# One layer of a hybrid encoder on one core: the order of the mix's plain halves, the slots of the late embeddings, and the steps at which finished quarters are passed on

## The chip, the core and the metric

The kernel runs on one core of a Trainium2 chip. The metric is the device time of one execution in microseconds (us); lower is better. The times of the runs of the kernel before are given as their median, and one more execution was taken with the hardware profiler: all rows shown below come from it. Engine names: PE is TensorE (matmuls and transposes), DVE is VectorE, ACT is ScalarE, POOL is GpSimd, SP is SyncE, whose queue issues most of the loads.

## What is computed

All in float32, for 512 tokens of width 2048, one layer:

```
qA|kA|vA|qB|kB|vB = x @ w_in
A = windowed attention, 8 heads, with sinks        B = dilated attention, 8 heads, three patterns
mix = concat(rms_norm(A), rms_norm(B)) @ w_o
h   = layer_norm(alpha * x + mix, ln1)
ff  = square(relu(h @ w1)) @ w2                    # 2048 -> 8192 -> 2048
ple = (p @ w_ple) * sigmoid(h @ w_ple_gate)
out = layer_norm(alpha * h + ff + ple, ln2)
```

## The kernel before

**Tiles.** Each float32 product is made of three matmuls: both operands are split into a high and a low part (wh, wl of the weights, s1h, s1l and so on of the features), ACT making the high part by a rounding copy and DVE the low part by a subtraction (lines 87 and 88 for weights, 433 and 434, put, for features). One matmul takes 128 x 128 features and 128 x 512 weights into a PSUM bank.

**Stages.** Attention and projections go first; the heads' results are scaled by a spread norm factor (line 327, after PE's line 307) and stored in DRAM as y_d (line 329). Then the embeddings of the first two column groups (embed(0), embed(1)) are made. The first half of the mix's columns is done by plain, a direct product: plain(nh, kh) adds column quarter nh's part from feature half kh, four steps of 24 matmuls, lines 458 to 460. Feature half 0 is head group A, whose tiles are s1 and s7 (key 21), feature half 1 is head group B, s2 and s4. They are loaded back from y_d by y_block (line 445) into tiles qh of 128 x 1024 in slots of tag g; y_sums makes the further sums s5, s6, s3 that the Strassen products want. plain_out (line 472) adds alpha * x and collects the row statistics.

The second half of the mix, the gate, W1 in eight passes n and W2 in four times two (m, c) run through strassen: seven products p, each of four steps k of twelve matmuls (lines 648 to 651), into three double banks a, b and c. STEPS, ENDS and FIRST5 are the lists of (p, k) in order; FIRST5, the gate's, begins with (5, 0). factor makes each step's weights from up to four loads wr, wq, wk (tags r, q, k with 4, 2 and 4 slots; hold=True puts one of them, wg, in tag g), and lines 600, 605, 617 and 618 are its sums. When a product ends, quarters copies the bank (line 664) or adds it to the quarter's tile c (line 666), and when the quarter is done calls done at once: for the mix mixed, which adds alpha * x and, when a row half is whole, runs norm_rows (lines 697 and 685: normalisation, transposes, stores h_d); for W1 squared, which transposes (line 786), squares, and stores the feature tiles f through POOL and ACT (s_d, line 791). After the mix come embed(2) and embed(3), whose result tiles pe and input tile pr stand in tag q, and then the gate.

**Order.** A scheduler places the instructions of each engine; the order in the program is its main guide, with the slots of each tag and the dependencies. Each engine then runs its own queue in that order. residual(th, n) is called between steps of a W1 pass: it loads zn, sg, pl, gb (lines 752 and 754) into tag g and combines them (lines 758 to 767). Slots: r 4, q 2, k 4, wh 3, wl 3, c 3, g 4.

## Time and profile before

| | us |
|---|---|
| median of 3 runs | 2300.74 (2296.46 to 2301.38) |
| profiled execution | 2308.33 |
| its span, first to last instruction | 2306.6 |
| PE busy | 2162.6 (94%) |
| DVE busy | 1633.1 (71%) |
| ACT busy | 1061.5 (46%) |
| mean granted clock of PE, share of full | 0.972 |
| mean DMA rate | 190 GB/s |

The profiled execution's own time is 1.7 us above its span. A busy PE is counted whatever clock it has been granted, so at the lower clock the same matmuls fill more time. The steps of the mix lie from 520 to 720, normalisation, embeddings and the gate's beginning from 720 to 797, W1 from 960 to about 1640, W2 from there.

### The profile page before, as it was taken

The page shows a single profiled execution, that of the slowest core. Times are in us where ns is not written, and L with a number is a line of the kernel's source. Part 1 is how long each engine was busy: PE and PEld are TensorE (multiplying, and loading weights), DVE is VectorE, ACT ScalarE, POOL GpSimd, SP SyncE. Part 2 cuts the span into 40 slices and gives each one's busy share as a digit, 9 for nine tenths or more (in the row PEclk, how much of TensorE's full clock was granted, in tenths as well). Part 3 has the DMA queues.
Part 4 walks back from the last instruction along what each step waited for, and adds up shares of the span by engine and source line. Part 5 has one row for each costly group of instructions (what it writes and reads, how often), then busy time and mean ns, then how long its engine had stood idle before and what let it go on. Part 6 is the DMA issues. An engine that isn't in the chain of part 4 may idle for free.

```text
span 2306.6 us, 25695 instructions
## 1 busy us (share of the span) xinstructions
PE 2162.6 (94%) x9576; PEld 1753.4 (76%) x9576; DVE 1633.1 (71%) x1864; ACT 1061.5 (46%) x1287; POOL 115.1 (5%) x192
## 2 busy tenths in 40 slices
PE   8999999996996799999999999989899999999995
PEld 7888888875784588887887877767677787787784
DVE  7675655554686767776876876867767777777787
ACT  5454333442345444454554454445445555555331
POOL 0000000000001000000000000000011011011000
PEclk9999999998997899999999999999999999999998
DMA  6212422236657656566675675676678779678572
GB/s 224 75 65 84 154 73 83 73 106 213 201 184 262 208 182 213 184 233 208 233 245 193 237 246 187 233 242 237 204 192 249 216 193 281 183 212 280 176 244 101
DMA packets 134767, 438.79 MB, mean 190 GB/s; under 512 B 13777, under 2 KB 24033, under 8 KB 134641
## 3 DMA queue, kind: packets, MB, share of 16 engines
q1 hardware_dynamic: 100368, 316.45, 41.2%
q0 software_dynamic: 26336, 95.53, 14.4%
q10 hardware_dynamic: 7936, 25.17, 3.0%
q8 instruction: 75, 1.23, 0.2%
q14 instruction: 52, 0.42, 0.1%
HBM read 354.25 MB, written 82.84 MB: 189 GB/s over the span
## 4 chain that ended last, share of the span: by engine, by line
PE 61%; DMA 14%; DVE 11%; issue 11%; ACT 2%; POOL 0%; DVEq 0%; SPq 0%; ACTq 0%; POOLq 0%
DMA wr<-in_w 7%; PE a L651 7%; PE a L648 7%; PE a L650 7%; PE u L94 6%; PE u L96 6%; PE u L95 6%; DVE wl L88 5%; PE b L648 3%; PE b L651 3%; PE b L650 3%; PE c L651 2%; PE c L648 2%; PE c L650 2%; DMA qs<-s_d 2%
## 5 line engine op out<-in xcount | busy, mean ns | idle before, releaser
L87 ACT ACTIVATE wh<-wr 128x1024 fp32r<-128x1024 f32 (+1 forms) x400 | 415.8, 1043 | 585.1 <-PE a L650 224.6
L88 DVE TENSOR_TENSOR wl<-wr,wh 128x1024 fp32r<-128x1024 f32 (+1 forms) x400 | 477.7, 1198 | 249.4 <-ACT wh L87 241.5
L87 ACT ACTIVATE wh<-wk 128x1024 fp32r<-128x1024 f32 x152 | 161.0, 1060 | 189.4 <-PE a L650 93.5
L94 PE MATMUL u<-xh,wh 128*128 128x512 f32 x576 | 228.0, 396 | 5.8 <-ACT xh L74 5.8
L88 DVE TENSOR_TENSOR wl<-wk,wh 128x1024 fp32r<-128x1024 f32 x152 | 184.9, 1220 | 61.4 <-ACT wh L87 61.2
L96 PE MATMUL u<-xh,wl 128*128 128x512 f32 x576 | 226.2, 393 | 0.0
L95 PE MATMUL u<-xl,wh 128*128 128x512 f32 x576 | 225.7, 392 | 0.0
L600 DVE TENSOR_TENSOR wk<-wr,wk 128x1024 f32<-128x1024 f32 x76 | 93.0, 1224 | 114.0 <-DMA wr<-in_w 102.4
L648 PE MATMUL b<-wh,s5h 128*128 128x512 f32 x304 | 121.9, 401 | 31.6 <-ACT wh L87 31.6
L94 PEld LDWEIGHTS u<-xh,wh 128*128 128x128 f32 x576 | 108.9, 189 | 27.6 <-ACT xh L74 5.8
L96 PEld LDWEIGHTS u<-xh,wl 128*128 128x128 f32 x576 | 108.7, 189 | 22.9
L95 PEld LDWEIGHTS u<-xl,wh 128*128 128x128 f32 x576 | 108.9, 189 | 22.4 <-DVE xl L75 0.4
L651 PE MATMUL b<-wl,s5h 128*128 128x512 f32 x304 | 121.5, 400 | 3.3 <-DVE wl L88 3.3
L651 PE MATMUL c<-wl,s2h 128*128 128x512 f32 x304 | 121.1, 398 | 3.6 <-DVE wl L88 3.3
L651 PE MATMUL a<-wl,s7h 128*128 128x512 f32 x304 | 122.2, 402 | 1.9 <-DVE wl L88 1.9
L648 PE MATMUL a<-wh,s7h 128*128 128x512 f32 x304 | 121.4, 399 | 2.7 <-ACT wh L87 2.2
L651 PE MATMUL b<-wl,s3h 128*128 128x512 f32 x304 | 120.1, 395 | 3.7 <-DVE wl L88 3.6
L648 PE MATMUL c<-wh,s2h 128*128 128x512 f32 x304 | 121.7, 400 | 0.0
L651 PE MATMUL a<-wl,s1h 128*128 128x512 f32 x304 | 120.2, 395 | 1.4 <-DVE wl L88 1.4
L650 PE MATMUL c<-wh,s2l 128*128 128x512 f32 x304 | 121.3, 399 | 0.0
L648 PE MATMUL a<-wh,s4h 128*128 128x512 f32 x304 | 120.5, 396 | 0.9 <-DVE c L666 0.6
L650 PE MATMUL a<-wh,s7l 128*128 128x512 f32 x304 | 121.2, 399 | 0.0
(296 smaller groups left out, 4661.1 us busy)
## 6 DMA issues: line engine op xcount, KB each, us to landing
wr<-in_w SPq DMA_DIRECT2D x196, 512.0 KB, 4.3
wr<-in_w_in SPq DMA_DIRECT2D x64, 512.0 KB, 3.6
wq<-in_w SPq DMA_DIRECT2D x64, 512.0 KB, 4.0
wk<-in_w POOLq DMA_DIRECT2D x64, 512.0 KB, 5.0
qs<-s_d SPq DMA_DIRECT2D x56, 512.0 KB, 5.0
z_d<-ev POOLq DMA_DIRECT2D x42, 512.0 KB, 7.2
wr<-in_w_o SPq DMA_DIRECT2D x32, 512.0 KB, 4.0
s_d<-f POOLq DMA_DIRECT2D x32, 512.0 KB, 4.8
```

The costliest lines, as they stand in the source:

```text
L87: nc.scalar.activation(hi, t, AF.Copy)
L88: nc.vector.tensor_tensor(lo, t, hi.bitcast(F32), op=ALU.subtract)
L94: nc.tensor.matmul(o, wh, ah, start=start, stop=False)
L95: nc.tensor.matmul(o, wh, al, start=False, stop=False)
L96: nc.tensor.matmul(o, wl, ah, start=False, stop=stop)
L600: nc.vector.tensor_tensor(t4[k], get(b21, k, 2, "r"), t2[k], op=ALU.subtract)
L648: nc.tensor.matmul(o, sh[:, i, x], wh[:, c], start=first and k == 0 and j == 0, stop=False, skip_group_check=skip)
L650: nc.tensor.matmul(o, sl[:, i, x], wh[:, c], start=False, stop=False, skip_group_check=skip)
L651: nc.tensor.matmul(o, sh[:, i, x], wl[:, c], start=False, stop=k == 3 and j == 1, skip_group_check=skip)
```

## The change

Four edits, with all they need:

- **Plain halves.** Before, plain(0,0) and plain(0,1) filled one set of banks, then plain(1,0) and plain(1,1) another. Now plain(0,0) and plain(1,0), which need only feature half 0, come first and are read out at once (alpha * x plus the sum, line 475); plain(0,1) and plain(1,1) start their banks anew and are added on top (line 477), which makes eight DVE operations more. hd.values comes after one step of plain(0,0) and not two. The y tiles of this stage take slots of tag c (3, which the attention's pairs also use) and not g; s7 is now made in y_sums.
- **Late embeddings.** embed(2) and embed(3) write tiles pe in tag g, and pr takes a slot of s1h; both were in q.
- **Finished quarters.** quarters has wait=2: the call of done is kept in a list and made two steps later (for the mix's second half wait is 0, at once). In norm_rows ha[g, 2] and ha[g, 3] change places.
- **W2's first product group** (m = c = 0) has hold=False.

The core of the diff:

```diff
-    def y_block(g, i):
-        x = block("qh")
+    def y_block(g, i, tag="g"):
+        x = block("qh", tag)
...
-                    first, end = kh == k == j == 0, kh == j == 1 and k == 3
+                    first, end = k == j == 0, j == 1 and k == 3
...
+            if kh == 0:
+                zs[th, nh] = pair("xt", "g")
+                x_load(th, nh, zs[th, nh])
+            z = zs[th, nh]
             for i in range(2):
-                nc.vector.scalar_tensor_tensor(z[:, i], z[:, i], ALPHA, o[2 * th + i], op0=ALU.mult, op1=ALU.add)
-            take_stats(th, nh, z)
+                if kh == 0:
+                    nc.vector.scalar_tensor_tensor(z[:, i], z[:, i], ALPHA, o[2 * th + i], op0=ALU.mult, op1=ALU.add)
+                else:
+                    nc.vector.tensor_tensor(z[:, i], z[:, i], o[2 * th + i], op=ALU.add)
+            if kh:
+                take_stats(th, nh, z)
...
-    plain(0, 0, o, range(2))
+    plain(0, 0, o, range(1))
     ssB = hd.values(V, ssB, oB)
-    plain(0, 0, o, range(2, 3))
+    plain(0, 0, o, range(1, 2))
     rB = rms_stats(ssB)
-    plain(0, 0, o, range(3, 4))
+    plain(0, 0, o, range(2, 4))
+    plain_out(0, 0, o)
     rms_scale(oB, rB, 8)
+    o = [bank() for _ in range(NQ)]
+    plain(1, 0, o)
+    plain_out(1, 0, o)
...
+    o = [bank() for _ in range(NQ)]
     plain(0, 1, o, range(2))
...
-    plain_out(0, o)
+    plain_out(0, 1, o)
...
-    plain(1, 0, o)
-    for g in range(2):
-        x, y = y_block(g, 0), y_block(g, 2)
-        nc.vector.tensor_tensor(x, x, y, op=ALU.subtract)
-        put(sy[g], 7, x)
     plain(1, 1, o)
-    plain_out(1, o)
+    plain_out(1, 1, o)
...
+            for w in list(after):
+                w[0] -= 1
+                if w[0] == 0:
+                    after.remove(w)
+                    w[1]()
...
-    def quarters(done, tags={}):
+    after = []
+
+    def quarters(done, tags={}, wait=2):
...
-            if p in LAST:
+            if p in LAST and wait:
+                after.append([wait, lambda: done(*q, c[q])])
+            elif p in LAST:
                 done(*q, c[q])
...
-                r = pair("pr", "q")
+                r = s_tile("pr", "s1h", (P, 2, S))
...
-        embed(g, rest[0], pt_bank, "q")
+        embed(g, rest[0], pt_bank, lambda th: pair("pe", "g"))
...
-            strassen(lambda k, q, m=m, c=c: w2[m, c, q, k], sf, read if more else last_sum(c), True, mid,
+            strassen(lambda k, q, m=m, c=c: w2[m, c, q, k], sf, read if more else last_sum(c), m + c > 0, mid,
```

The scheduler's order at three places, by engine. In the kernel after, the lines 648, 650 and 651 are 663, 665 and 666, line 666 is 684, lines 685 and 786 are 705 and 806.

**PE and DVE between the plain halves.** u are the banks, s the spread of the norm factor; s1 and s7 are tiles of feature half 0, s2 and s4 of half 1. PE before:

```order
L460 MATMUL u<-wl,s7h 128x512
L307 MATMUL s<-ident,r 128x128 x4
L458 MATMUL u<-wh,s2h 128x512 x2
L459 MATMUL u<-wh,s2l 128x512
L460 MATMUL u<-wl,s2h 128x512
L459 MATMUL u<-wh,s2l 128x512
L460 MATMUL u<-wl,s2h 128x512
```

PE after:

```order
L460 MATMUL u<-wl,s7h 128x512
L307 MATMUL s<-ident,r 128x128 x4
L458 MATMUL u<-wh,s1h 128x512
L459 MATMUL u<-wh,s1l 128x512
L460 MATMUL u<-wl,s1h 128x512
L458 MATMUL u<-wh,s1h 128x512
```

DVE before, behind the scaling:

```order
L434 TENSOR_TENSOR s2l_4521<-qh_4518,s2h_4520 128x1024
L434 TENSOR_TENSOR s4l_4527<-qh_4524,s4h_4526 128x1024
L434 TENSOR_TENSOR s2l_4533<-qh_4530,s2h_4532 128x1024
L434 TENSOR_TENSOR s4l_4539<-qh_4536,s4h_4538 128x1024
L517 TENSOR_TENSOR qh_4602<-qh_4602,qh_4604 128x1024
L88 TENSOR_TENSOR wl_4658<-wr_4655,wh_4657 128x1024
```

DVE after, from the end of the scaling:

```order
L327 SCALAR_TENSOR_TENSOR o_4057<-o_4057,vec_90,rb_4504 128x512 x2
L88 TENSOR_TENSOR wl_4615<-wr_4612,wh_4614 128x1024
L88 TENSOR_TENSOR wl_4689<-wr_4686,wh_4688 128x1024
L434 TENSOR_TENSOR s2l_4661<-qh_4658,s2h_4660 128x1024
L434 TENSOR_TENSOR s4l_4667<-qh_4664,s4h_4666 128x1024
L434 TENSOR_TENSOR s2l_4673<-qh_4670,s2h_4672 128x1024
L88 TENSOR_TENSOR wl_4719<-wr_4716,wh_4718 128x1024
L475 SCALAR_TENSOR_TENSOR xt_4642<-xt_4642,u_4518 128x512
L434 TENSOR_TENSOR s4l_4679<-qh_4676,s4h_4678 128x1024
L475 SCALAR_TENSOR_TENSOR xt_4642<-xt_4642,u_4519 128x512
L475 SCALAR_TENSOR_TENSOR xt_4646<-xt_4646,u_4520 128x512
L475 SCALAR_TENSOR_TENSOR xt_4646<-xt_4646,u_4521 128x512
```

On PE, a product from s1 stands behind L307 where one from s2 stood. On DVE the reads of plain(1,0)'s banks (L475, banks u_4518 to u_4521) stand among the splits of the four B tiles (L434, s2l and s4l); three of them are behind the fourth split.

**PE at the normalisation behind the mix.** b is the double bank of the gate's product 5 (with s5h) after the mix's product 3 (with s3h); pt are the banks of transposes (L685, L705) and of the embeddings (L94 to L96). Before:

```order
L648 MATMUL b<-wh,s3h 128x512
L650 MATMUL b<-wh,s3l 128x512
L651 MATMUL b<-wl,s3h 128x512
L685 MATMUL pt<-ident,xt 128x128 x8
L685 MATMUL pt<-ident,c_5116 128x128 x8
L685 MATMUL pt<-ident,xt 128x128 x8
L685 MATMUL pt<-ident,c_5228 128x128 x8
L94 MATMUL pt<-wh,ph 128x512
L95 MATMUL pt<-wl,ph 128x512
```

After, from the end of the third of the gate's first steps:

```order
L663 MATMUL b<-wh,s5h 128x512
L665 MATMUL b<-wh,s5l 128x512
L666 MATMUL b<-wl,s5h 128x512
L663 MATMUL b<-wh,s5h 128x512
L665 MATMUL b<-wh,s5l 128x512
L666 MATMUL b<-wl,s5h 128x512
L705 MATMUL pt<-ident,xt 128x128 x2
L663 MATMUL b<-wh,s5h 128x512
L705 MATMUL pt<-ident,xt 128x128 x6
L665 MATMUL b<-wh,s5l 128x512
L705 MATMUL pt<-ident,c_5124 128x128 x8
L705 MATMUL pt<-ident,xt 128x128 x4
```

The three first steps of the gate's product 5 have come ahead of the transposes of xt and c, and the fourth stands among them.

**PE in a W1 pass, step (7, 3).** a is the bank of product 7; the transposes pt<-ident,c are those of quarter (0, 1). Before:

```order
L648 MATMUL a<-wh,s7h 128x512
L650 MATMUL a<-wh,s7l 128x512
L651 MATMUL a<-wl,s7h 128x512
L648 MATMUL a<-wh,s7h 128x512
L650 MATMUL a<-wh,s7l 128x512
L651 MATMUL a<-wl,s7h 128x512
L648 MATMUL a<-wh,s7h 128x512
L650 MATMUL a<-wh,s7l 128x512
L786 MATMUL pt<-ident,c_8439 128x128 x8
L651 MATMUL a<-wl,s7h 128x512
```

After:

```order
L663 MATMUL a<-wh,s7h 128x512
L665 MATMUL a<-wh,s7l 128x512
L666 MATMUL a<-wl,s7h 128x512
L663 MATMUL a<-wh,s7h 128x512
L665 MATMUL a<-wh,s7l 128x512
L666 MATMUL a<-wl,s7h 128x512
L663 MATMUL a<-wh,s7h 128x512
L665 MATMUL a<-wh,s7l 128x512
L666 MATMUL a<-wl,s7h 128x512
L806 MATMUL pt<-ident,c_8447 128x128 x8
L663 MATMUL c<-wh,s2h 128x512
```

The transposes have moved from behind eight of the step's twelve matmuls to behind all twelve.

## Rows read from the trace of the kernel before

**Rows 1.** The page's head.

```profile
span 2306.6 us, 25695 instructions
```

**Rows 2.** Stretches: length, busy (x) of five engines, clock, DMA share, GB/s.

```profile
546.00:570.00 24.00, 4.15 (x16) 2.85 (x15) 9.18 (x12) 4.67 (x5) 2.16 (x4) 0.60 0.85 292
...
720.00:750.00 30.00, 9.69 (x37) 7.11 (x38) 21.97 (x39) 14.16 (x23) 4.64 (x8) 0.58 0.68 239
750.00:797.00 47.00, 30.80 (x110) 22.36 (x110) 35.98 (x32) 20.58 (x24) 0.00 (x0) 0.79 0.65 223
```

**Rows 3.** PE at the plain halves: start, us, instruction [idle before <-releaser].

```profile
545.65 0.39 PE L460 MATMUL u<-wl,s7h 128*128 128x512 f32 x1
545.88 1.05 PE L307 MATMUL s<-ident,r 128*128 128x128 f32 x8
566.74 1.22 PE L458 MATMUL u<-wh,s2h 128*128 128x512 f32 x2 [19.81 <-ACT s2h L433]
...
569.02 0.63 PE L459 MATMUL u<-wh,s2l 128*128 128x512 f32 x1
569.45 0.63 PE L460 MATMUL u<-wl,s2h 128*128 128x512 f32 x1
```

**Rows 4.** DVE there.

```profile
548.08 5.38 DVE L327 SCALAR_TENSOR_TENSOR o<-o,vec,rb 128x512 f32<-128x512 f32 x8
```

**Rows 5.** SP there.

```profile
554.77 15.12 SPq L445 DMA_DIRECT2D qh<-y_d  x6
```

**Rows 6.** Tile qh, 480 to 640: how long its loads take.

```profile
DMA to landing us min/median/max: 3.5/5.1/12.0
```

**Rows 7.** PE at the normalisation and the gate's first product.

```profile
734.39 1.94 PE L685 MATMUL pt<-ident,xt 128*128 128x128 f32 x8 [15.70 <-DVE xt L697]
...
774.95 0.79 PE L648 MATMUL b<-wh,s5h 128*128 128x512 f32 x1 [11.49 <-ACT wh L87]
```

**Rows 8.** The chain that ended last, by time: start, us, what.

```profile
766.57 6.18 DMA ple_d<-pe
772.77 3.41 DMA wq<-in_w_gate
```

**Rows 9.** Waits of PE, 1040 to 1660: us in total, times, longest.

```profile
PE b L648 <- ACT wh L87: 17.1, 2, 9.0
PE pt L786 <- DVE c L666: 15.5, 8, 2.6
PE a L648 <- ACT wh L87: 2.2, 2, 1.5
PE a L651 <- DVE wl L88: 1.4, 3, 0.5
```

**Rows 10.** PE at a wait of W1's third pass.

```profile
1243.62 1.73 PE L786 MATMUL pt<-ident,c 128*128 128x128 f32 x8 [2.62 <-DVE c L666]
```

**Rows 11.** DVE ahead of that wait.

```profile
1240.08 1.23 DVE L600 TENSOR_TENSOR wk<-wr,wk 128x1024 f32<-128x1024 f32 x1 [2.44 <-DMA wr<-in_w]
...
1242.35 1.21 DVE L666 TENSOR_TENSOR c<-c,b 128x1024 f32<-128x1024 f32 x1
```

**Rows 12.** Stretches of W1, then the passage to W2; columns of rows 2.

```profile
1140.00:1170.00 30.00, 29.14 (x135) 23.48 (x134) 20.73 (x18) 14.59 (x16) 1.07 (x2) 1.00 0.58 192
1230.00:1260.00 30.00, 27.37 (x119) 21.82 (x118) 16.92 (x15) 13.53 (x15) 2.12 (x4) 0.94 0.59 193
1550.00:1600.00 50.00, 44.66 (x177) 34.16 (x178) 40.42 (x37) 26.25 (x28) 0.53 (x1) 0.92 0.60 197
1600.00:1665.00 65.00, 54.35 (x234) 43.73 (x233) 48.62 (x42) 31.72 (x36) 5.14 (x9) 0.92 0.72 245
```

**Rows 13.** The chain that ended last, at the last W1 pass.

```profile
1539.04 8.06 DMA gb<-in_lnb
```

**Rows 14.** PE at that pass.

```profile
1550.90 0.79 PE L648 MATMUL b<-wh,s5h 128*128 128x512 f32 x1 [9.03 <-ACT wh L87]
```

**Rows 15.** PE at W2's first product.

```profile
1643.02 0.80 PE L648 MATMUL b<-wh,s5h 128*128 128x512 f32 x1 [8.10 <-ACT wh L87]
```


## What was predicted

> **What bounds the kernel now.** I read the head of the page first: the span is 2306.6 us [rows 1], and the table of the section on time has TensorE (PE) busy for 2162.6 of it, so time can be won only where PE waits or runs at its lower clock. I looked for these in the view of stretches, then listed PE's waits, and followed each wait back through the engine that ended it. Four places hold nearly all that this change touches. At the plain halves of the mix PE stands for 19.81 us [rows 3]: its next product needs feature tiles of head group B, which go VectorE (DVE) to DRAM and back; the scaling runs 548.08 to 553.5 [rows 4], the loads are issued from 554.77 [rows 5], and one of them took 12.0 us where the median is 5.1 [rows 6]. At the normalisation PE stands for 15.70 us, and at the gate's first product for 11.49 us [rows 7]; of the 77 us from 720 to 797 it is busy for 9.69 + 30.80 [rows 2]. In the W1 passes it waits eight times, 15.5 us in all, for DVE's sum of a quarter (c, line 666) before it may transpose it [rows 9]. And at the last W1 pass and W2's first product it stands for 9.03 and 8.10 us [rows 14, 15]. After each long gap the matmuls follow each other at 0.43 us (569.02 to 569.45) and not at 0.23 (545.65 to 545.88) [rows 3], the lower of the two clock levels, 1.2 for 2.4 GHz; the mean granted clock of 546 to 570 is 0.60 [rows 2].
>
> The sum below is made on the profiled execution, 2308.33 us (1.7 beyond its span). The median of the runs shown, 2300.74, is 7.6 below it, and I take that off at the end.
>
> **A, the plain halves.** The order shows the part of plain(1,0) that needs only the first feature tiles (s1, s7) right behind L307, where plain(0,1) stood before. Four steps of 24 matmuls at 0.23 give 22 us of work, against a gap of 19.81; so the gap goes, and with it the slow matmuls behind it, which I count at 3.0 us (some fifteen, 0.2 each): -22.8. What is late next? First, plain(0,1)'s banks. They are read out by the new L475 operations of plain(1,0), and DVE's order has three of these behind s4l<-qh, whose tile waits for a free slot: the y tiles now share three slots of tag c, where before four of tag g held them. So the fourth load is issued only when the first tile is split. With T = 545.88, the loads go out near T+9; at 12.0 us each [rows 6] the first is there at T+21, its two splits take 2.3, the fourth load at 5.1 lands at T+28.4, and two splits and one read-out later (3.0) PE's second bank is free at T+31.4, against T+23 when PE has ended plain(1,0). That is 8.4 less the three matmuls that run ahead (0.7): 7.7. With 5.1 for all loads it is about 1, with 12.0 for all 15. I take 7.7 because the same weight loads of the k slots still go out beside the first three, and the fourth has less company; and 1.5 for the clock behind it. Second, y_sums passes one chain of loads through the same three slots, so the second step of plain(1,1) may find its weights late: no row shows this, its bounds are 0 and one load (5.1), and I take 3.5 and 1 for the clock. Third, hd.values now stands behind one step of plain(0,0) and not two, so PE may wait for its inputs; bounds 0 and the 5.5 us of the step that covered it; I take 2. Eight more DVE operations on 128x512 at about 0.67 each (5.38 for eight of line 327 [rows 4]) are 5.4 us that lie beside PE's 22 us of work and cost nothing; were DVE full there, they would cost that. A = -22.8 + 7.7 + 1.5 + 3.5 + 1 + 2 = -7.1, say -7. Ends: -20 (short loads, no late weights) and 0.
>
> A page weighs against the short loads. The Trainium skill, "DMA: Bandwidth & Descriptors", section "Issuing engines are not separate DMA queues", says that transfers started by different engines end up on the same sixteen DMA engines and interleave, so pulling the plain weights forward would lengthen the y loads beside them; by it all loads stay at 12.0 us and A would be about 0, the first rival below.
>
> **B, normalisation, late embeddings, first gate steps.** Before, wq for the gate's first step was asked for only after the embeddings' tiles (pe), which shared its two q slots, had been stored: the chain reads ple_d<-pe 6.18, then wq<-in_w_gate 3.41 [rows 8]. With pe in g slots and pr in s1h, SP asks for these weights during the mix, and PE has the first three gate steps (36 matmuls, 8.2 us) ahead of the transposes and the fourth among them. So the 11.49 goes. But DVE gets the gate's factors in the midst of the normalisation: nine operations on 128x1024 at 1.2 (as line 600 and line 666 [rows 11]), some 11 us, so the first of the late transposes comes near 745, not 734.39. Before: of 77 us 36.5 were not busy [rows 2], 15.70, 11.49 and some 9.3 in small gaps; the low clock cost about 10.5 (9.69 x 0.42 + 30.80 x 0.21, the shares by which the clock fell short). After: the first gap grows to 26.7 and takes in 8.2 of work, 18.5; of the small ones those around the gate's first step go with it (I count 2.6) and the fourth step's 2.7 fills others, 4 stay; clock 6.5. That is 29 for 47: B = -18. Ends: -26 (DVE does the factors while it would have waited anyway) and -8 (each gate step waits for the one free slot of wh and wl, two being held by the embedding's weights).
>
> **C, transposes later in W1.** The wait of two steps moves little, since the scheduler places the transposes itself: in each pass c01's stand at the end of step (7,3) and not four matmuls before it, 0.9 us later; one split is moved ahead of the line 600 that stands for a load at 1240.08 for 2.44 us, and before the sum at 1242.35 that PE waits for [rows 11]. So of waits like the 2.62 [rows 10] some 0.9 goes, about 7 us over the eight. The stretch with such a wait, 1230 to 1260, had a clock of 0.94; the one of the pass before, not busy for 30 - 29.14 = 0.86 us, had 1.00 [rows 12]; 30 x 0.06 is 1.8 us, and I count five waits of the longer kind. If the shortened ones cost as little as the short ones do now, 5 x 1.4 = 7 come back as well. With 1 for the other transposes, C = -15; ends -6 (clock not regained) and -23 (all).
>
> The clock half of this stands against a rule: the Trainium skill, "TensorE: Matmul & The Clock Gate", section "A second HAM failure mode: psum-queue depth-cycling", tells of a kernel in which PE's short idles between groups kept the clock swinging. By it C would be about -8 and the sum 7 us less; the stretch from 1140 with its short wait and a clock of 1.00 speaks against it here.
>
> **D, the last W1 pass.** There wq stood on SP behind four residual loads that wait for slots; the chain goes through gb, 8.06 us to landing [rows 13], then L761, then L617. In the new order wq is issued behind zn alone, some 3.6 us earlier, and L617 stands before L761 (1.3). The 9.03 [rows 14] falls to about 4, with 1 of clock; the slower q slots behind it (50 us with 44.66 busy, clock 0.92 [rows 12]) I leave as they are, and 1 is lost where sg, pl, gb come later. D = -5; ends -10 and +2.
>
> **E, W2's first half.** hold is off for m = c = 0, so wq is loaded into q slots instead of waiting for g slots behind the f tiles. The 8.10 [rows 15] and about 6.5 more of idle and clock go (1600 to 1665: 54.35 of 65 busy, clock 0.92 [rows 12]). Added: four loads of 512 KB beside PE, 3.4 us each as the gate's wq [rows 8], and a ring of two q slots as in the last W1 pass, whose stretch lost 50 - 44.66 = 5.3, less the 9.03's share that falls into it (0.9), and 50 x 0.08 = 4 by the clock; I take 8 less the 1.4 that the 9.03 left in that clock, 6.6. E = -8; ends -14 and 0.
>
> Sum: -7 - 18 - 15 - 5 - 8 = -53, so 2308.3 - 53 = 2255.3 on the profiled run and **2248** against the median. All good ends together give -93, all bad ones -12.
>
> **Rivals.** (1) The slots of tag c cost the whole gap: loads at 12.0 us throughout, A = 0: 2255. For it speak the DMA share of 0.85 in that stretch [rows 2]; against it the median of 5.1. (2) The gate's factors delay the normalisation by all that the earlier gate steps gain: B = 0, 2266; with (1), 2273. Against it: the 11.49 has a cause that the change takes away. (3) Transposes hardly earlier than their sum: C = -6, D = 0, 2262; with (1) and (2) together 2287. (4) Covers hold everywhere: A -20, B -24, C -20, D -8, E -12: 2217. (5) Slower: a quarter lies in one of three slots of tag c until its transposes are done. If these really come two steps later (24 matmuls at 0.23, 5.5 us), the slot comes free as much later, ACT's copy of the next quarter waits for it, and PE for the bank that this copy empties. Two quarters held up in each of eight passes cost 16 x (5.5 - s), s being the slack of the slots, and C's 15 are not won: with no slack 2248 + 15 + 88 = 2351, and slower than before from a slack below about 3. Against it: the order moves the transposes by 0.9 us and not by 5.5, and PE's list of waits in W1 has four kinds, none of them for a copy of a quarter [rows 9].
>
> **How the numbers follow.** Forecast, 2236 to 2258, 0.45; rivals (1) to (3), alone or in pairs, 2258 to 2285, 0.30; (4), 2212 to 2236, 0.15; three or more together, 2285 to 2296, 0.03; within 0.2% of 2300.74 (4.6 us, about what a measurement here can tell from no change) 0.03; slower 0.04. The likeliest is 2248. The range of 2216 to 2283 leaves out what is below (0.04) and above (0.12). Faster 0.93, same 0.03, slower 0.04.
>
> **What would show it.** A is right if PE has no gap at L307 and one of 5 to 10 us with DVE's L475 as its releaser about 23 us later; wrong if there is none, or if it reaches 15. B: the gate's first product before the transposes, the first late transpose near 745 plus the shift of A, and no wait of 11 us for wh. C: the eight waits fall from 15.5 to about 8, with stretches of W1 at a clock near 1.00; PE waiting for ACT's copy of a quarter in every pass would be rival 5. D and E: gaps of 4 and 0 to 4 where 9.03 and 8.10 stood. The prediction is wrong as a whole if PE's sum of waits falls by less than 25 us.

## The result and the profile after

The changed kernel takes 2276.45 us (median of 4 runs, 2271.84 to 2281.18) against 2301.06 (4 runs): a ratio of 0.9897, 95% interval 0.9867 to 0.9927. So it is faster by 1.0%, 24.6 us, where 2.3%, 53 us, was forecast; the time lies within the range of 2216 to 2283, near its slow end, but the gain is less than half the forecast. The profiled execution took 2280.34 us, its span 2278.6.

To see where the 28.0 us between the two profiled spans lie (3.4 more than between the medians), I cut both at the same places of the program: the start of W1, the start of the first step of its eighth pass, the end of that pass, and the end of W2's first product group. The first step of product 1 (a<-wh,s1h) marks each. Stretches of before, with columns as in [rows 2]:

```profile
0.00:937.80 937.80, 869.07 (x3945) 712.10 (x3946) 603.24 (x927) 404.86 (x615) 21.25 (x43) 0.96 0.45 152
937.80:1524.20 586.40, 574.19 (x2569) 467.45 (x2568) 441.90 (x391) 289.20 (x306) 30.84 (x58) 0.99 0.65 219
1524.20:1624.10 99.90, 86.43 (x370) 67.85 (x370) 74.53 (x67) 50.64 (x55) 4.79 (x9) 0.93 0.73 247
1624.10:1718.80 94.70, 82.59 (x346) 65.93 (x345) 62.47 (x54) 40.52 (x42) 9.62 (x14) 0.95 0.69 203
1718.80:2306.60 587.80, 550.29 (x2353) 440.11 (x2351) 451.00 (x429) 276.23 (x272) 48.65 (x68) 0.98 0.71 212
```

The same five of after:

```profile
0.00:908.70 908.70, 869.19 (x3944) 710.97 (x3945) 607.50 (x935) 404.90 (x615) 21.22 (x43) 0.98 0.45 154
908.70:1504.60 595.90, 575.65 (x2569) 465.53 (x2568) 440.32 (x391) 289.36 (x307) 30.83 (x58) 0.99 0.64 215
1504.60:1604.90 100.30, 89.03 (x370) 68.36 (x369) 75.94 (x68) 50.05 (x55) 4.79 (x9) 0.95 0.71 241
1604.90:1694.70 89.80, 82.41 (x346) 65.54 (x345) 61.26 (x53) 40.49 (x42) 9.61 (x14) 0.96 0.81 243
1694.70:2278.60 583.90, 550.05 (x2353) 441.83 (x2351) 451.05 (x429) 275.95 (x272) 48.64 (x68) 0.98 0.71 213
```

Their lengths differ by -29.1, +9.5, +0.4, -4.9 and -3.9. Up to W1 the change brings even more than the forecast's A and B together (-25). The first seven W1 passes, from which term C wanted 15 us back, have become 9.5 us longer: PE stands 595.90 - 575.65 = 20.3 us there, 12.2 before. Against the forecast that is 24.5 us, about as much as the whole shortfall. The other terms nearly cancel: D and E fell short by 5 and 3, the stretch up to W1 was 4 better, and the rest of the kernel, whose order on PE, DVE and ACT is the same in both, came out 4 shorter in this execution (in the runs below it lies between 582.4 and 591.0).

Which waits these are, the list of PE's waits for the six passes after the first says (us in total, times, longest). Before, it had one kind, the transposes' wait for the sum c; after, it has two:

```profile
PE pt L786 <- DVE c L666: 12.1, 6, 2.6
...
PE a L666 <- DVE wl L88: 13.5, 9, 3.3
PE pt L806 <- DVE c L684: 6.7, 5, 1.5
```

The transposes' wait has fallen, as forecast, from 12.1 to 6.7 us. A new wait of 13.5 us has come in its place: in step (6, 1) of each pass (12.1 us of it, 1.3 to 3.3 each) PE's third matmul needs wl, the low part that DVE splits (L88).

### The profile page after: what moved, and what is told of

Read it like the earlier page. It is cut to its first block, busy times and chain, and to the rows that moved or that the text cites. A ratio compares the mean times of both kernels' runs of the same rounds, so it can differ in the third digit from the quotient of the medians.

```text
span 2278.6 us, 25699 instructions
## 1 busy us (share of the span) xinstructions
PE 2166.3 (95%) x9576; PEld 1752.2 (77%) x9576; DVE 1636.1 (72%) x1872; ACT 1060.7 (47%) x1287; POOL 115.1 (5%) x192
## 4 chain that ended last, share of the span: by engine, by line
PE 66%; DMA 12%; issue 10%; DVE 10%; ACT 2%; POOL 0%; DVEq 0%; SPq 0%; ACTq 0%; POOLq 0%
PE a L666 8%; PE a L663 8%; PE a L665 8%; PE u L94 6%; PE u L96 6%; PE u L95 6%; DVE wl L88 4%; PE b L666 3%; PE b L663 3%; PE b L665 3%; DMA wr<-in_w 3%; PE c L666 3%; PE c L663 3%; PE c L665 3%; DMA s_d<-f 2%
## 5 line engine op out<-in xcount | busy, mean ns | idle before, releaser
L88 DVE TENSOR_TENSOR wl<-wr,wh 128x1024 fp32r<-128x1024 f32 (+1 forms) x400 | 478.7, 1199 | 239.8 <-ACT wh L87 233.0
L94 PE MATMUL u<-xh,wh 128*128 128x512 f32 x576 | 227.4, 395 | 5.9 <-ACT xh L74 5.9
L96 PE MATMUL u<-xh,wl 128*128 128x512 f32 x576 | 225.7, 392 | 0.0
L88 DVE TENSOR_TENSOR wl<-wk,wh 128x1024 fp32r<-128x1024 f32 x152 | 185.1, 1221 | 56.4 <-ACT wh L87 56.3
L663 PE MATMUL b<-wh,s5h 128*128 128x512 f32 x304 | 122.4, 403 | 14.9 <-DVE c L684 8.4
L666 PE MATMUL a<-wl,s6h 128*128 128x512 f32 x304 | 122.0, 401 | 12.1 <-DVE wl L88 12.1
L94 PEld LDWEIGHTS u<-xh,wh 128*128 128x128 f32 x576 | 108.6, 188 | 27.6 <-ACT xh L74 5.9
L663 PE MATMUL a<-wh,s6h 128*128 128x512 f32 x304 | 121.7, 400 | 7.8 <-ACT ev L884 4.6
L96 PEld LDWEIGHTS u<-xh,wl 128*128 128x128 f32 x576 | 108.4, 188 | 22.8
L665 PE MATMUL a<-wh,s1l 128*128 128x512 f32 x304 | 120.7, 397 | 4.7 <-DVE s1l L434 4.7
L663 PE MATMUL a<-wh,s1h 128*128 128x512 f32 x304 | 121.2, 399 | 1.7 <-ACT wh L87 1.7
```

The source lines that it names most:

```text
L88: nc.vector.tensor_tensor(lo, t, hi.bitcast(F32), op=ALU.subtract)
L94: nc.tensor.matmul(o, wh, ah, start=start, stop=False)
L96: nc.tensor.matmul(o, wl, ah, start=False, stop=stop)
L663: nc.tensor.matmul(o, sh[:, i, x], wh[:, c], start=first and k == 0 and j == 0, stop=False, skip_group_check=skip)
L665: nc.tensor.matmul(o, sl[:, i, x], wh[:, c], start=False, stop=False, skip_group_check=skip)
L666: nc.tensor.matmul(o, sh[:, i, x], wl[:, c], start=False, stop=k == 3 and j == 1, skip_group_check=skip)
```

## One pass of W1 after the change

The fourth pass, which starts at 1161.4, shows how it comes about (the same pass of before, from 1185.5, is the one that [rows 10] calls the third). PE, SP and DVE of after in order of time; "idle before" stands in brackets with what ended it. PE:

```profile
1187.04 0.39 PE L665 MATMUL a<-wh,s6l 128*128 128x512 f32 x1
1189.55 0.50 PE L666 MATMUL a<-wl,s6h 128*128 128x512 f32 x1 [2.12 <-DVE wl L88]
```

SP, that issues the residual's four loads (L772, L774) and the weights:

```profile
1175.17 0.33 SPq L772 DMA_DIRECT2D pl<-ple_d  x1
1181.11 0.38 SPq L774 DMA_DIRECT2D gb<-in_lnb  x1
1181.59 0.89 SPq L80 DMA_DIRECT2D wq<-in_w  x2
```

DVE:

```profile
1182.64 1.23 DVE L778 TENSOR_TENSOR sg<-sg,pl 128x1024 f32<-128x1024 f32 x1 [1.28 <-DMA pl<-ple_d]
1187.67 0.69 DVE L781 SCALAR_TENSOR_TENSOR zn<-zn,gb 128x512 f32<-128x512 f32 x1 [3.80 <-DMA gb<-in_lnb]
1188.28 1.22 DVE L88 TENSOR_TENSOR wl<-wk,wh 128x1024 fp32r<-128x1024 f32 x1
```

DVE in the same pass of before:

```profile
1206.67 1.22 DVE L88 TENSOR_TENSOR wl<-wk,wh 128x1024 fp32r<-128x1024 f32 x1
1209.79 1.29 DVE L761 SCALAR_TENSOR_TENSOR zn<-zn,gb 128x512 f32<-128x512 f32 x2 [1.90 <-DMA gb<-in_lnb]
```

SP comes to the load of gb after pl, at 1175.5, and can issue it only at 1181.11: it takes the fourth slot of tag g, and that comes free when the last of the f tiles, which sit in the same four slots, has been stored. SP's own list of waits names it, in the six passes of after and of before; behind it stands the load of gb in the pass of before:

```profile
SPq L774 <- DMA s_d<-f: 29.7, 6, 5.5
...
SPq L754 <- DMA s_d<-f: 13.7, 6, 5.0
...
1202.39 0.38 SPq L754 DMA_DIRECT2D gb<-in_lnb  x1
```

The f tiles come from the transposes, so they are later by what the transposes are later: the last store is issued 11.2 us behind the pass's first step (1172.57 behind 1161.4), where it was 10.2 (1195.66 behind 1185.5). That is the smaller part of the delay. The store also takes longer to land, 8.5 us for 6.7 in this pass, and gb goes out when it has landed: 19.7 us behind the first step, where it was 16.9. Over the six passes gb goes out 3.2 us later on average, 1.0 by the later store and 2.2 by its longer way; why the store takes longer is not shown. The weights' load wq stands behind gb on SP (1181.59). On DVE the product zn * gb (L781) stands ahead of the split wl<-wk (1188.28) that PE waits for, and it waits 3.80 us for gb. In the kernel before that split was ahead of the product (1206.67 and 1209.79): two places in DVE's order had changed, and the prediction read only the one in front of PE's sum, not this one. So there are three readings, and the runs were to tell them apart: the split's place on DVE, SP's stand at gb with the weights behind it, or the late f tiles as such.

## Experiments

A table of all of them comes at the end of the section. The times are medians; every ratio is to the kernel before, run on the same chip.

**Wait of two steps taken out of W1.**

```diff
-        strassen(lambda k, q, n=n: w1[n, q, k], sh, quarters(squared), between=mid)
+        strassen(lambda k, q, n=n: w1[n, q, k], sh, quarters(squared, wait=0), between=mid)
```

> The changed kernel with the two steps' wait taken out of W1 alone (quarters called with wait=0 there); all else as changed. In the changed kernel six W1 passes (the second to the seventh) have gaps and clock losses of 33.4 us together where the kernel before has 23.5, and the new part of it is a wait of PE for a split (wl, L88) that stands in DVE's order behind L781, which waits for gb. Theory 1 (the wait moved L781 ahead of that split): the split stands ahead of L781 again, the wait of 1.3 to 3.3 us per pass goes, the passes are as long as before, and the time is 2276 - 10 = 2266. Theory 2 (the f tiles themselves come late and hold their slots): also about 2266, and this run can't tell the two apart. Theory 3 (W1 lost for another reason, such as traffic or slots left over from the new stages ahead): no change, 2276, and the wait for the split stays.

Measured: 2266.2, ratio 0.9844 (0.9808 to 0.9879). The first seven passes take 581.0 us (595.9 in the changed kernel); of the wait for the split nothing is left, and SP's wait at gb is down to 12.5 us in the six passes:

```profile
PE pt L806 <- DVE c L684: 11.0, 6, 2.6
```

So the wait of two steps, as the change has it, costs 10 us and does not bring 15. Theory 3 is out.

**The wait of two steps alone, on the kernel before.** Its core:

```diff
+            for w in list(after):
+                w[0] -= 1
+                if w[0] == 0:
+                    after.remove(w)
+                    w[1]()
...
-            if p in LAST:
+            if p in LAST and wait:
+                after.append([wait, lambda: done(*q, c[q])])
+            elif p in LAST:
                 done(*q, c[q])
```

> The kernel before with nothing but the wait of two steps for finished quarters (gate and W1; the mix as before). The prediction's step C says -15. Theories 1 and 2: W1's second to seventh pass lose 10 us more than before, L781's counterpart stands one split earlier, the whole is 2306 to 2312. Theory 3: W1 as before or better, 2287 to 2301.

Measured: 2312.7, ratio 1.0055 (1.0036 to 1.0074), 0.7 above the range of theories 1 and 2. Alone it makes the kernel 11 us slower, and by the same wait (lines are others here):

```profile
PE a L656 <- DVE wl L88: 11.9, 7, 2.4
PE pt L795 <- DVE c L673: 8.9, 6, 1.7
```

Two runs from opposite sides give the same cost, 10 and 11 us. PE's and DVE's order in the first seven passes is the same in the changed kernel, in this run and in the run with hold kept (below), which take 595.9, 594.8 and 594.0 us there; and it is the same in the kernel before, in the run without the wait and in the two runs with one of the first edits alone: 586.5, 581.0, 581.9 and 580.8. So the cost stands clear of what single executions of one order differ by.

**Later steps of the residual put back on DVE.**

```diff
-        for i, step in zip((6, 10, 13), residual(n % 2, n // 2)):
+        for i, step in zip((6, 16, 18), residual(n % 2, n // 2)):
```

> The changed kernel with the residual's second and third step of each W1 pass called at steps 16 and 18 of the pass, not 10 and 13, so that DVE's order has L781 (which waits for gb) behind two more splits; the wait of two steps for finished quarters stays. Theory 1 (order on DVE): PE's wait for the split in step (6,1) goes from all passes, what the wait=2 was to bring to the transposes stays, W1's six passes lose 15 to 20 us and not 33, and the time is 2258 to 2264. Theory 2 (the f tiles come late, gb's slot comes late): the wait only moves to the next split behind L781, and the time stays at 2272 to 2280.

Measured: 2285.3, ratio 0.9931 (0.9912 to 0.9949): 9 us slower than the changed kernel and outside both expected ranges. Theory 1 is out in its simple form. The wait has grown, and now a sum stands ahead of the split. PE's waits in the six passes, then SP and DVE in the fourth:

```profile
PE a L666 <- DVE wl L88: 21.7, 6, 5.5
PE pt L806 <- DVE c L684: 3.5, 2, 2.2
...
1183.64 0.38 SPq L774 DMA_DIRECT2D gb<-in_lnb  x1
1184.12 0.89 SPq L80 DMA_DIRECT2D wq<-in_w  x2
...
1191.94 1.23 DVE L615 TENSOR_TENSOR wq<-wr,wq 128x1024 f32<-128x1024 f32 x1 [5.61 <-DMA wq<-in_w]
1193.08 1.22 DVE L88 TENSOR_TENSOR wl<-wk,wh 128x1024 fp32r<-128x1024 f32 x1
```

The product with gb no longer stands there, but L615 waits for wq, which SP issued right behind gb, at 1184.12. So gb holds up two queues, one behind the other: whichever is taken away, the other still stands.

**gb issued by POOL.**

```diff
-            nc.sync.dma_start(t["gb"], bass.AP(tensor=lnb.tensor, offset=lnb.offset + n * S,
+            nc.gpsimd.dma_start(t["gb"], bass.AP(tensor=lnb.tensor, offset=lnb.offset + n * S,
```

> The changed kernel (wait of two steps kept) with the load of gb issued by POOL, behind the stores of the f tiles whose slot it takes, and not by SP. DVE's order is unchanged: L781, which needs gb, still stands ahead of the split that PE waits for. In the second run the wait did not go when DVE's order was put right; it moved to a sum (L615) whose load wq stands on SP behind gb. Theory SP (SP stands at gb for a slot, and the weights' loads stand behind it; L781 is only the second in the row): the weights come some 6 us earlier, but L781 still holds the split: the wait shrinks a little at most, 2272 to 2277. Theory DVE alone (L781's place is the whole cause, and the second run was slower because its later steps held slots longer): 2276, the same within 2, too; the run after this one tells the two apart. If gb lands later by POOL's queue, the wait grows and the time is 2280 or more.

Measured: 2285.3, ratio 0.9938 (0.9917 to 0.9959), the case that was to be 2280 or more: the wait grows. POOL, too, waits for the end of the stores of f (the row's 7.98 us) and issues gb as late in the pass as SP did, 19.7 us behind its first step; it lands 7.7 us after its issue by the median and not 6.8, and DVE's L781 stands in front of the split as in the changed kernel:

```profile
1184.90 0.72 POOL L774 DMA_DIRECT2D gb<-in_lnb  x1 [7.98 <-DMA s_d<-f]
...
1191.99 0.69 DVE L781 SCALAR_TENSOR_TENSOR zn<-zn,gb 128x512 f32<-128x512 f32 x1 [4.58 <-DMA gb<-in_lnb]
1192.60 1.22 DVE L88 TENSOR_TENSOR wl<-wk,wh 128x1024 fp32r<-128x1024 f32 x1
```

SP's queue being free is worth nothing as long as DVE stands for gb.

**Both at once.** The two diffs above together, with the wait of two steps.

> Both at once: gb issued by POOL, and the residual's later steps called at 16 and 18, so that neither SP's weights nor DVE's split stands behind gb; wait of two steps kept. Theory SP and DVE together (two queues in a row behind one slot): the wait of PE for the split in step (6,1) goes in all passes, six passes lose 15 to 20 us and not 33 or 42, and the time is 2258 to 2266. Theory of late f tiles as such (anything that takes their slots is late, sg and pl as well): the wait stays at 2 us or more per pass, 2272 or above.

Measured: 2266.8, ratio 0.9856 (0.9833 to 0.9879). With gb out of SP's queue and L781 behind the split, PE's waits in the six passes are:

```profile
PE pt L806 <- DVE c L684: 7.5, 5, 2.0
PE a L666 <- DVE wl L88: 2.8, 5, 1.8
```

The first seven passes take 582.0 us. Each of the two edits alone cost 9 us, together they win 10 (the time is 0.8 above the range expected): in the changed kernel the loss was a load that waits for a slot, with both the weights' queue and the split's queue behind it. The third reading, late f tiles as such, is out: their last store is issued 11.2 us behind the pass's first step here too, and gb goes out as late, 17.8 to 20.1 us behind it (18.3 to 19.9 in the changed kernel). One thing differs beside the two edits: the scheduler placed the product sg * pl (L778) behind two sums (L615) here and ahead of them in the run with the late steps alone. What that place alone is worth was not run.

**No wait of two steps, gb by POOL; the same with the late steps; the late steps alone.** Three runs to see what the wait of two steps is worth where gb is not in the way.

> The first run's kernel (wait=0 in W1) with gb issued by POOL. If SP's stand at gb costs something without the wait of two steps too (the loads of the ring behind it, and with them the sums that PE's transposes wait for, 12.1 us in eight waits), the time falls from 2266 to 2256 to 2262. If gb has slack there, it stays at 2266 within 3.

> No wait of two steps in W1, gb issued by POOL, the residual's later steps called at 16 and 18: the sixth run's kernel with wait=0. If the two queues behind gb's slot are the whole of W1's loss, it equals the sixth run within 3 us (2264 to 2270), the wait of two steps being worth at most the 0.9 us per pass of the shifted transposes. If the wait of two steps does bring something once gb no longer stands in the way, this run is slower than the sixth by 5 us or more (2272 and up); if it only does harm, faster (2255 to 2262).

> The first run's kernel (wait=0 in W1, gb by SP) with the residual's later steps called at 16 and 18. It completes the table of three choices in W1: wait of two steps or none, gb by SP or POOL, later steps at 10 and 13 or at 16 and 18. If late steps cost because they hold their slots longer, the first seven W1 passes grow from 581 to about 590, as they grew from 596 to 605 with the wait of two steps: 2275. If with gb early enough (wait=0) the late steps are free, 581 stays: 2266.

Measured: 2275.4, 2277.0 and 2290.3; ratios 0.9891 (0.9863 to 0.9919), 0.9891 (0.9853 to 0.9929), 0.9949 (0.9931 to 0.9968). None came as its first expectation said; the second came as its other case (2272 and up), the first and the third lie outside all that was expected. The three choices give these lengths of the first seven W1 passes, in us from the profiled executions, with the whole kernel's median behind each:

| | later steps at 10, 13: gb by SP | gb by POOL | at 16, 18: gb by SP | gb by POOL |
|---|---|---|---|---|
| no wait | 581.0; 2266.2 | 590.2; 2275.4 | 612.6; 2290.3 | 597.5; 2277.0 |
| two steps | 595.9; 2276.45 (the change) | 600.8; 2285.3 | 605.0; 2285.3 | 582.0; 2266.8 |

So the wait of two steps is worth -15.5 in one setting (597.5 to 582.0) and +14.9 in another (581.0 to 595.9); by the medians -10 and +10. By the medians both other choices hang on where the later steps are called. At 10 and 13, with L781 ahead of the split or just behind it, the wait of two steps costs 10 us by either queue, and POOL costs 9. At 16 and 18 the wait saves 5 (not clear of noise) and 10, and POOL saves 13 and 18. In the slowest, 612.6, the waits of PE are many and small; DVE's own wait for a weight is the third line:

```profile
PE pt L806 <- DVE c L684: 14.8, 6, 2.7
PE a L666 <- DVE wl L88: 12.5, 19, 1.3
...
DVE wq L615 <- DMA wq<-in_w: 32.7, 18, 4.5
```

Nineteen waits for a split of 0.7 us on average: the residual's five later operations (L781 twice, L786 twice, L787) then stand close together in DVE's order among the splits of four steps, and the sums L615, two of which now stand ahead of them, wait for their weights, which they don't in the run without the wait and with the steps at 10 and 13. These waits of PE are about half of the loss (in the six passes PE stands 27.8 us for 11.1); for the other half PE's busy time is longer, at a mean granted clock of 0.98 for 1.00. The packing alone is not the cause: the same run with gb by POOL has the same order on PE and DVE and takes 597.5. Why this order costs more than the others was not taken further, so no rule for it is given here.

**Each of the first two edits alone.** The plain halves alone (embeddings, wait, hold and norm_rows as before), then the embeddings' slots alone on the kernel before; their diffs, the first to the changed kernel, the second to the one before.

```diff
-                r = s_tile("pr", "s1h", (P, 2, S))
+                r = pair("pr", "q")
...
-        embed(g, rest[0], pt_bank, lambda th: pair("pe", "g"))
+        embed(g, rest[0], pt_bank, lambda th: pair("pe", "q"))
...
-    def quarters(done, tags={}, wait=2):
+    def quarters(done, tags={}, wait=0):
...
-                x = ha[g, 2]
+                x = ha[g, 3]
...
-            strassen(lambda k, q, m=m, c=c: w2[m, c, q, k], sf, read if more else last_sum(c), m + c > 0, mid,
+            strassen(lambda k, q, m=m, c=c: w2[m, c, q, k], sf, read if more else last_sum(c), True, mid,
```

```diff
-                r = pair("pr", "q")
+                r = s_tile("pr", "s1h", (P, 2, S))
...
-        embed(g, rest[0], pt_bank, "q")
+        embed(g, rest[0], pt_bank, lambda th: pair("pe", "g"))
```

> The first edit alone: the plain halves' new order and their slots; late embeddings in q, no wait of two steps, hold=True and the order in norm_rows as before. The prediction's step A says -7 (ends -20 and 0). From the changed kernel's trace (stretch from 500 to the mix's Strassen part: 30.0 us of gaps and clock before, 15.2 after) it should be about -15: 2286. If the mix behind it gives some back (slots of tag c, late tiles), 2290 to 2295.

> The second edit alone on the kernel before: pe of embed(2) and embed(3) in tag g, pr in a slot of s1h; plain halves, finished quarters, norm_rows' order and hold as before. The prediction's step B says -18. From the changed kernel's trace (mix's Strassen part to the end of the gate: 52.4 us of gaps and clock before, 39.2 after, where a new wait for s1l in the gate's product 1 gives 6 back) it should be -13: 2287 to 2288. If the rival of step B holds without the other edits (DVE's gate factors inside the normalisation eat the gain), 2296 to 2301.

Measured: 2281.9, ratio 0.9928 (0.9908 to 0.9947), and 2282.7, ratio 0.9910 (0.9884 to 0.9937). Each alone is worth 19 to 20 us, some 4 to 5 more than was expected. By the start of W1 they are 16.3 and 19.8 us ahead of the kernel before (921.5 and 918.0 for 937.8); the change with both is ahead by 29.1, so 7 us are lost where they meet. The place is the gate's first step of product 1. PE and DVE of the changed kernel:

```profile
762.50 0.79 PE L665 MATMUL a<-wh,s1l 128*128 128x512 f32 x1 [4.73 <-DVE s1l L434]
...
760.09 1.22 DVE L615 TENSOR_TENSOR wq<-wr,wq 128x1024 f32<-128x1024 f32 x1 [5.13 <-DMA wr<-in_w_gate]
761.23 2.35 DVE L434 TENSOR_TENSOR s1l<-ha,s1h 128x1024 fp32r<-128x1024 f32 x2
```

The split s1l stands on DVE behind a sum that waits 5.13 us for a weight; with the embeddings' edit alone no wait of PE in that stretch is longer than 0.4 us. The wait is 4.7 of the 7; the stretch of the gate that holds it, 752.0 to 831.4, also has a granted clock of 0.96, where it is 1.00 with either edit absent.

**hold kept in W2's first group.** The rest as changed.

```diff
-            strassen(lambda k, q, m=m, c=c: w2[m, c, q, k], sf, read if more else last_sum(c), m + c > 0, mid,
+            strassen(lambda k, q, m=m, c=c: w2[m, c, q, k], sf, read if more else last_sum(c), True, mid,
```

> The changed kernel with hold=True kept in W2's first product group. If the prediction's step E is right in mechanism, a wait of about 8 us for wg stands at W2's first product again and W2's first group is 5 to 8 us longer: 2281 to 2285. Rival: in the changed kernel the g slots come free in another order, the wait for wg is short, and the edit is worth nothing: 2276 within 2.

Measured: 2280.6, ratio 0.9915 (0.9887 to 0.9942), 4 us slower than the changed kernel, which is not clear of noise by itself. W2's first group takes 93.0 us (89.8 changed), and its wait is there again:

```profile
1620.93 0.79 PE L663 MATMUL b<-wh,s5h 128*128 128x512 f32 x1 [9.77 <-ACT wh L87]
```

All runs together are clearer: in the five kernels with hold in that group it takes 92.7 to 94.7 us, in the eight without it 82.9 to 89.8, some 6 less on average.

All runs in one table. The passage is from the start of W1's eighth pass to the end of W2's first group.

| kernel | median us | ratio (95%) | start of W1 | seven passes | passage |
|---|---|---|---|---|---|
| before | 2301.06 | | 937.8 | 586.5 | 194.5 |
| changed | 2276.45 | 0.9897 (0.9867 to 0.9927) | 908.7 | 595.9 | 190.1 |
| wait=0 in W1 | 2266.2 | 0.9844 (0.9808 to 0.9879) | 909.2 | 581.0 | 189.9 |
| later steps late | 2285.3 | 0.9931 (0.9912 to 0.9949) | 905.3 | 605.0 | 187.7 |
| before, wait of two steps | 2312.7 | 1.0055 (1.0036 to 1.0074) | 941.3 | 594.8 | 192.3 |
| hold kept | 2280.6 | 0.9915 (0.9887 to 0.9942) | 908.9 | 594.0 | 193.8 |
| gb by POOL | 2285.3 | 0.9938 (0.9917 to 0.9959) | 909.1 | 600.8 | 189.4 |
| gb by POOL, late steps | 2266.8 | 0.9856 (0.9833 to 0.9879) | 908.1 | 582.0 | 182.1 |
| wait=0, gb by POOL | 2275.4 | 0.9891 (0.9863 to 0.9919) | 905.0 | 590.2 | 186.0 |
| plain halves alone | 2281.9 | 0.9928 (0.9908 to 0.9947) | 921.5 | 581.9 | 191.5 |
| embeddings alone | 2282.7 | 0.9910 (0.9884 to 0.9937) | 918.0 | 580.8 | 191.1 |
| wait=0, gb by POOL, late steps | 2277.0 | 0.9891 (0.9853 to 0.9929) | 906.0 | 597.5 | 186.2 |
| wait=0, late steps | 2290.3 | 0.9949 (0.9931 to 0.9968) | 905.3 | 612.6 | 181.2 |

Two of these beat both kernels, the one without the wait in W1 (2266.2) and the one with gb by POOL and late steps (2266.8); their intervals don't tell them from each other. A median lies up to 9 us from its profiled execution, so the last three columns say where time went, and the ratio what the kernel is worth.

## Why the prediction came out as it did

**What was right.** The bound (places where PE stands), the mechanisms of A, B, D and E in the main, and the sign. A's wait stood where it was put. PE has no gap at L307, the stretch 546 to 570 is full (21.86 of 24 us busy at a clock of 1.00, for 4.15 at 0.60 in [rows 2]), and the one gap comes 22 us behind the spread. PE and DVE there, with SP's loads of the y tiles:

```profile
546.00:570.00 24.00, 21.86 (x97) 17.73 (x95) 11.34 (x13) 5.96 (x8) 2.17 (x4) 1.00 0.87 305
570.00:592.00 22.00, 18.86 (x69) 14.66 (x70) 17.77 (x17) 8.43 (x9) 0.00 (x0) 0.84 0.70 232
...
573.07 0.77 PE L458 MATMUL u<-wh,s2h 128*128 128x512 f32 x1 [5.21 <-ACT s4h L433]
...
570.00 1.23 DVE L434 TENSOR_TENSOR s2l<-qh,s2h 128x1024 fp32r<-128x1024 f32 x1 [0.20 <-ACT s2h L433]
571.15 1.22 DVE L88 TENSOR_TENSOR wl<-wr,wh 128x1024 fp32r<-128x1024 f32 x1
572.28 0.68 DVE L475 SCALAR_TENSOR_TENSOR xt<-xt,u 128x512 f32<-128x512 f32 x1
...
553.93 4.07 SPq L445 DMA_DIRECT2D qh<-y_d  x3
...
564.52 7.10 SPq L445 DMA_DIRECT2D qh<-y_d  x3
```

The view names ACT's s4h, but this product doesn't read it; the read-out L475, which ends at 572.96 and empties the product's bank, is the last thing ahead of PE's 573.07. It stands on DVE behind the split of the third B tile. The fourth load goes out at 564.52, when the first tile (landed at 562.1) has been split, as the slots of tag c made it. The size was off, 5.21 for 7.7, and the path was not quite the sum's: the sum had PE wait for its second bank, behind the fourth load, and it waited for the first, behind the third tile's split. The loads took 8.1, 13.1, 11.3 and 7.1 us, where the sum had 12.0 for the first and 5.1 for the fourth. Before, the same four had taken 10.8, 12.0, 10.1 and 11.2, so the 12.0 of [rows 6] was no odd one among them; the median of 5.1 comes from the later loads. That the size came near is in part luck. The late weights of plain(1,1) cost 1.8 for 3.5, hd.values 1.1 for 2. So A, -7 in the sum, is -16 by the start of W1 and -18.5 in the whole when alone. The Trainium skill, "DMA: Bandwidth & Descriptors", section "Issuing engines are not separate DMA queues", says that transfers started by different engines run on the same sixteen DMA engines and interleave. The prediction drew from it that A would be about 0; the loads above were on the whole not longer than before (40 us for 44 in all four), at a DMA share of 0.87 for 0.85, and no run here takes the weights' loads away from beside them.

B was sized right: -18 forecast, -19.8 alone at W1's start. The gate's factors stand in the normalisation as the order said. PE:

```profile
704.22 0.40 PE L666 MATMUL b<-wl,s3h 128*128 128x512 f32 x1
713.06 0.77 PE L663 MATMUL b<-wh,s5h 128*128 128x512 f32 x1 [8.45 <-DVE c L684]
...
716.38 0.80 PE L666 MATMUL b<-wl,s5h 128*128 128x512 f32 x1 [2.12 <-DVE wl L88]
...
732.22 0.44 PE L705 MATMUL pt<-ident,xt 128*128 128x128 f32 x2 [0.54 <-DVE xt L717]
```

PE's last product of the mix ends at 704.6, the first late transpose comes with DVE's normalisation at 732.2, 27.6 us later, where 26.7 was forecast; the gap of 15.70 [rows 7] is now 8.45, 2.12 and small ones, and the 11.49 is gone. What no step of the prediction had is the 7 us that A and B lose to each other in the gate's product 1. D: the 9.03 [rows 14] fell to 2.13, better than the 4 forecast, but the next steps wait for the two q slots, so idle time fell only from 99.90 - 86.43 = 13.5 to 11.3 us and PE's busy time rose from 86.43 to 89.03 for the same 370 records, though the mean granted clock is 0.95 for 0.93 (why is not shown): nothing for the -5. E: the 8.10 [rows 15] is gone, 4.56 of a wait for ACT's copy came in its place: -4.9 by the stretch, -4 by the run and some -6 by all runs together, for -8.

**What was wrong: term C.** "The wait of two steps moves little ... C = -15" counted what the shift of 0.9 us saves at PE's transposes, and there it was right (12.1 to 6.7 us). It missed the shift's other end. The f tiles that come of the transposes sit in the four g slots into which the residual's loads go. The sum moved one DVE split ahead of the sum that PE waits for and gave it as a gain; it did not list the split that the product L781 had passed in the same row of DVE, nor the queue behind gb on SP. In numbers: C was to be -15, and is +10 by the run that takes the wait out, +11 by the run that adds it to the kernel before. Rival 5 spoke of held slots but of the wrong tag (c, and ACT's copies): PE's list of waits shows no wait for a copy of a quarter in the six passes. The clock half of C (7 us) did not come back either: the mean granted clock of the six passes is 0.99 in both kernels. What it hangs on stays open: it is 1.00 in the run without the wait, and 1.00 too in the run with hold kept, which has the same order there and stands as long (21.6 us for the changed kernel's 20.3). The Trainium skill, "TensorE: Matmul & The Clock Gate", section "A second HAM failure mode: psum-queue depth-cycling", tells of a kernel in which PE's short idles between groups kept the clock swinging. The half that stayed lost agrees with it; the 1.00 with hold kept, beside waits of up to 2.3 us, does not.

In the profiled executions the expected 53 thus went as follows: 25 lost in C, 5 in D, 3 to 4 in E and 7 where A and B meet, against 9 to 11 more from A, 2 from B and 4 in stretches of unchanged order, which is noise.

## What to carry to other kernels

When a step is delayed, follow its tile to the slot it frees: list every load that takes that slot, every queue that issues such a load with what stands behind it, and every operation that reads the load with what stands behind that. A slot that comes free 3 us later can hold two in-order queues one behind the other, and mending one of them alone may cost time. Price edits alone as well as together: two that are worth 19 us each gave 29 together by the same point, and one whose direct effect was right (half the transposes' wait gone) was the one that cost.

## What had not been expected

The places of five small operations on DVE move a W1 stretch between 581.0 and 612.6 us, 5%, though DVE is busy for only 440 of 596 us there in the changed kernel: a busy share of three quarters was no sign of slack here, where each split has to be ready at its own time. The load of gb took 6.8 us to land by the median when SP issued it and 7.7 when POOL did (six each, the changed kernel and the one with gb by POOL). Other runs don't bear this out as a matter of the queue: 7.4 by SP in the kernel before, 7.3 by POOL in the run with the late steps.
